# Sparse attention on Trainium2: negated scores, probabilities scaled on GpSimd alone, and one compressed softmax for both token tiles

## The chip, the cores and the metric

The kernel runs on one core of one Trainium2 chip. The metric is the device time of one execution in microseconds (us), the median of several runs. In the profile PE is TensorE (PEld its weight loads), DVE is VectorE, ACT is ScalarE, POOL is GpSimd.

## The reference

The program is three layers over 256 tokens of width 1024: a block of four mixers with an MLP, a retention layer with a gated feed-forward, and a layer of native sparse attention (NSA) with another feed-forward. The change touches only the attention of the NSA layer. With 16 heads in 4 groups, and for each block of 128 queries, it computes:

```
s = einsum(q, kc) + bias                        # 15 compressed keys
p_c = masked_softmax(s, dist_c >= 0);  o_c = einsum(p_c, vc)
s = einsum(q, k_sel) + bias                     # selected blocks
p_s = masked_softmax(s, mask_s);       o_s = einsum(p_s, v_sel)
s = einsum(q, kwin) + bias                      # window
p_w = masked_softmax(s, mask_w);       o_w = einsum(p_w, vwin)
o = gate0 * o_c + gate1 * o_s + gate2 * o_w
```

`masked_softmax` subtracts the row's maximum, takes the exponential and divides by the row's sum (with a floor against rows without any key). At 256 tokens every selected block and the whole window are in reach, so both are plain causal attention with different keys.

## The kernel before, in words

Weights are streamed from HBM as float32 and split into a rounded part (`whi`, L230 on ScalarE) and a remainder (`wlo`, L233 on VectorE), and every projection takes three matmuls (L245 to L247). The function `nsa` first projects keys, values, queries and gates and compresses keys and values; `NSA_ORDER` writes down in which order these pieces and the first score units are issued. Within that, the framework's planner orders the instructions of each engine when the kernel is built, so an engine's order in the trace is not always the order of the source. Each engine then works its own queue in order.

The 16 heads are two pairs of groups (`pair`, 8 heads each: `a` picks the group, `r` one of its four heads). A unit is (pair, token tile `t`, heads `r0` to `r0+nr`, branch `b`: selected or window). There are 12 units, numbered 0 to 11: per pair one of token tile 0 with 4 heads per group and 128 keys, and two of token tile 1 with 2 heads per group and 256 keys, each for both branches. For each unit:

- `u_scores`: TensorE writes the scores into two PSUM banks (L1402, L1403, L1405). VectorE adds the bias table `tz`, writes the sum to SBUF and takes the row maximum in one instruction (L1413, followed by a read of its accumulator), negates the maxima (L1416), ScalarE takes the exponential with the row's sum (L1419), VectorE inverts the sum and multiplies it with the gate (L1421, L1423), and the probabilities are scaled by this row factor (L1425): the half `a = 0` on VectorE, the half `a = 1` on GpSimd.
- `u_weights`: TensorE transposes the probabilities, 4 transposes per half (L1435); ScalarE copies the first half out of PSUM (L1440), VectorE the second (L1438).
- `u_outputs`: TensorE multiplies with the values (L1452); with the window branch it adds the compressed branch from the same bank (L1457), and the result is split into `oT` (L238, L239).

The loop at the end of `nsa` issues in each turn the transposes of unit i, the scores of a later unit, and the outputs of unit i - 1. The compressed softmax (`cmp_softmax`, L1351 to L1377) runs once per pair and token tile: step `S` of the order for pair 0, turn 1 of the loop for pair 1. Its scaling, L1376, is on VectorE. `cmp_weights` (L1379) transposes its result.

After the last unit `project_back` multiplies `oT` with `w_no`.

Of the kernel before, what the change touches and what calls it, by code (L numbers as in the profile page):

```python
# [12 lines left out]
F32 = mybir.dt.float32  # L13
# [3 lines left out]
OP = mybir.AluOpType  # L17
# [6 lines left out]
NEG = -1e30  # L24
# [184 lines left out]
class Kernel:  # L209
# [977 lines left out]
    def nsa(self, inp, xq_pool):  # L1187

        nc, I = self.nc, self.I
        mm = nc.tensor.matmul  # L1190
        rb = self.rb
        with ExitStack() as es:
            cp = self.pool(es, "nc_")
# [3 lines left out]
            tz = cp.tile([128, 16, T], F32, name="tz")  # L1197
# [150 lines left out]
                nc.vector.tensor_scalar(g, g, 1.0, 0.5, op0=OP.add, op1=OP.mult)  # L1348


            def cmp_softmax(pair, t):  # L1351
                nk = 15 if t else 7
                s = cp.tile([128, 8, 32], F32, name=f"sc{pair}{t}")
                nc.gpsimd.memset(s, 0.0)
                sv = s[:, :, 15 - nk:15]

                ps = self.bank()[:, :8 * nk].rearrange("p (r a n) -> p r a n", r=4, a=2)
                for r in range(4):
                    mm(ps[:, r], qT[:, pair * 4 + r, t * 128:(t + 1) * 128], kcz[:, pair, :, 15 - nk:],
                       start=True, stop=True)  # L1360
                for a in range(2):
                    h = pair * 8 + a * 4
                    nc.vector.tensor_tensor(sv[:, a * 4:a * 4 + 4, :], ps[:, :, a, :],
                                            tz[:, h:h + 4, 0:16 * (nk - 1) + 1:16], op=OP.add)
                m = self.st.tile([128, 8], F32, tag="m8", name="m8")
                nc.vector.tensor_reduce(m, sv, AX.X, OP.max)
                nc.vector.tensor_scalar(m, m, -1e25, None, op0=OP.max)
                nc.vector.tensor_tensor(sv, sv, m[:, :, None].to_broadcast([128, 8, nk]), op=OP.subtract)
                nc.scalar.activation(sv, sv, AF.Exp)
                z = self.st.tile([128, 8], F32, tag="z8", name="z8")  # L1370
                nc.vector.tensor_reduce(z, sv, AX.X, OP.add)
                nc.vector.tensor_scalar(z, z, float(np.finfo(np.float32).tiny), None, op0=OP.max)
                rz = self.st.tile([128, 8], F32, tag="rz8", name="rz8")
                nc.vector.reciprocal(rz, z)
                nc.vector.tensor_tensor(rz, rz, gate[:, t, 0, pair * 8:pair * 8 + 8], op=OP.mult)
                nc.vector.tensor_tensor(sv, sv, rz[:, :, None].to_broadcast([128, 8, nk]), op=OP.mult)  # L1376
                return s  # L1377

            def cmp_weights(pair, t, s):  # L1379
                p = self.bank()[:, :256]  # L1380
                for a in range(2):
                    nc.tensor.transpose(p[:, a * 128:(a + 1) * 128],
                                        s[:, a * 4:a * 4 + 4, :].rearrange("p r n -> p (r n)"), self.ident)
# [8 lines left out]
            def u_scores(pair, t, r0, nr, b):  # L1392
                L = 128 * (t + 1)
                ts = slice(t * 128, (t + 1) * 128)
                i = next(nth) % 4
                s = (sp if i < 3 else more[0]).tile([128, 2, nr, L], F32, tag="s", name="s")
                sc = [self.bank().rearrange("p (r k) -> p r k", r=nr) for _ in range(2)]

                for a, i in itertools.product(range(2), range(nr)) if t else [(a, i) for i in range(nr) for a in range(2)]:
                    if t:  # L1400
                        q = qs[a][:, pair, r0 + i]
                        mm(sc[a][:, i, :], q, kh[a][:, b, pair], start=True, stop=False)  # L1402
                        mm(sc[a][:, i, :], q, kl[a][:, b, pair], start=False, stop=True)  # L1403
# [18 lines left out]
                gb = gate[:, t, 1 + b, pair * 8:pair * 8 + 8].rearrange("p (a r) -> p a r", a=2)  # L1422
# [23 lines left out]
            def u_outputs(pair, t, r0, nr, b, pts):  # L1446
# [23 lines left out]
                "S": lambda: sc.update({0: [cmp_softmax(0, t) for t in range(2)]}),  # L1470
# [19 lines left out]
            for i in range(len(units) + 1):  # L1490
                if i < len(units):
                    pts[i] = u_weights(*units[i], ss.pop(i))
                score()
                if i == 0:
                    score()
                if i in (0, 4):
                    for t in range(2):
                        cmp_weights(i // 4, t, sc[i // 4][t])
                if i == 1:
                    sc[1] = [cmp_softmax(1, t) for t in range(2)]  # L1500
                if i:
                    u_outputs(*units[i - 1], pts.pop(i - 1))

# [15 lines left out]
```

## Time and profile before

| | us |
|---|---|
| median of 3 runs | 1227.83 (1225.94 to 1228.5) |
| the profiled execution, its own time | 1227.54 |
| its span in the profile | 1225.8 |
| the attention stage in it | about 940 to 1005.3 |

The granted TensorE clock was full (0.996 in the mean). The span is the time from the first to the last instruction; the stretches below are in us from its start.

### The profile page before, as it was taken

The numbers are of one execution on the slowest core, as the hardware profiler recorded it, in microseconds if no ns is written. First come the engines' busy times: TensorE is split into PE (matmuls) and PEld (weight loads), VectorE is DVE, ScalarE is ACT, GpSimd is POOL, SyncE is SP. The second block draws the span as 40 slices with busy tenths as digits, with TensorE's granted clock in tenths as the row PEclk, the third lists the DMA queues.
The fourth block names the chain that finished last, engine by engine and source line by source line (L and its number), as shares of the span: only waits on it lengthen the run. The fifth ranks groups of instructions, "written<-read, shape, count | busy, mean of one in ns | idle before, by whom it ended". The sixth has DMA issues, their size and how long they took to land.

```text
span 1225.8 us, 20004 instructions
## 1 busy us (share of the span) xinstructions
PE 1202.4 (98%) x7872; PEld 1074.7 (88%) x7872; DVE 775.8 (63%) x1335; ACT 632.2 (52%) x1031; POOL 84.0 (7%) x85
## 2 busy tenths in 40 slices
PE   8999999999999999999999999999999999999997
PEld 6999999997889998899778889999789767899996
DVE  7756866557645557656556655456688977645453
ACT  5544665436544455543545544445577776544441
POOL 1002202100000000012000000000100220000000
PEclk8999999999999999999999999999999999999999
DMA  7554355546455566554446265556654216555560
GB/s 243 188 185 140 104 188 162 167 155 205 163 179 186 184 195 209 190 191 161 161 147 224 98 207 185 187 188 211 200 186 158 71 60 211 177 188 187 182 199 35
DMA packets 60782, 210.22 MB, mean 172 GB/s; under 512 B 7120, under 2 KB 9808, under 8 KB 60560
## 3 DMA queue, kind: packets, MB, share of 16 engines
q1 hardware_dynamic: 60688, 208.95, 52.1%
q8 instruction: 62, 1.02, 0.3%
q14 instruction: 32, 0.26, 0.1%
HBM read 207.84 MB, written 1.08 MB: 170 GB/s over the span
## 4 chain that ended last, share of the span: by engine, by line
PE 85%; DVE 6%; DMA 3%; ACT 3%; issue 1%; POOL 1%; SPq 0%; DVEq 0%; POOLq 0%; ACTq 0%
PE b L245 26%; PE b L246 26%; PE b L247 26%; DVE wlo L233 2%; PE b L408 1%; ACT whi L230 1%; DMA raw<-w_up 1%; PE b L537 1%; DVE s L1413 1%; ACT s L1419 1%; DMA wng<-w_ng 1%; PE b L569 1%; PE b L1081 1%; DMA raw<-w_fi 1%; PE b L588 1%
## 5 line engine op out<-in xcount | busy, mean ns | idle before, releaser
L233 DVE TENSOR_TENSOR wlo<-raw,whi 128x1024 fp32r<-128x1024 f32 (+3 forms) x432 | 473.5, 1108 | 310.4 <-ACT whi L230 307.4
L230 ACT ACTIVATE whi<-raw 128x1024 fp32r<-128x1024 f32 (+1 forms) x384 | 401.3, 1051 | 438.8 <-PE b L246 193.7
L245 PE MATMUL b<-xh,whi 128*128 128x256 f32 x1504 | 428.7, 285 | 0.0
L246 PE MATMUL b<-xl,whi 128*128 128x256 f32 x1504 | 424.6, 282 | 0.0
L247 PE MATMUL b<-xh,wlo 128*128 128x256 f32 x1504 | 424.6, 282 | 0.0
L245 PE MATMUL b<-whi,xh 128*128 128x512 f32 (+1 forms) x752 | 295.8, 395 | 3.0 <-ACT xh L205 2.1
L246 PE MATMUL b<-wlo,xh 128*128 128x512 f32 (+1 forms) x752 | 293.6, 391 | 0.1
L247 PE MATMUL b<-whi,xl 128*128 128x512 f32 (+1 forms) x752 | 291.8, 389 | 0.0
L245 PEld LDWEIGHTS b<-xh,whi 128*128 128x128 f32 x1504 | 287.1, 191 | 3.4 <-issue 2.0
L246 PEld LDWEIGHTS b<-xl,whi 128*128 128x128 f32 x1504 | 287.1, 191 | 1.1
L247 PEld LDWEIGHTS b<-xh,wlo 128*128 128x128 f32 x1504 | 287.1, 191 | 0.0
L245 PEld LDWEIGHTS b<-whi,xh 128*128 128x128 f32 x752 | 141.7, 189 | 36.7 <-ACT xh L205 5.1
L246 PEld LDWEIGHTS b<-wlo,xh 128*128 128x128 f32 x752 | 141.9, 189 | 30.6 <-DVE wlo L233 2.2
L247 PEld LDWEIGHTS b<-whi,xl 128*128 128x128 f32 x752 | 141.7, 188 | 29.5 <-DVE xl L206 0.3
L389 POOL TENSOR_TENSOR rstd<-ms,mhalf 128x1 f32<-128x1 f32 x22 | 14.1, 642 | 692.3 <-DVE ms L387 692.3
L206 DVE SCALAR_TENSOR_TENSOR xl<-b,gc,xh 128x128 fp32r<-128x128 f32 x112 | 36.7, 348 | 19.8 <-ACT xh L205 17.8
L205 ACT ACTIVATE xh<-b,gc 128x128 fp32r<-128x128 f32 x112 | 38.3, 368 | 20.1 <-PE b L408 15.2
L1419 ACT ACTIVATE s<-s,nm 128x128 f32<-128x128 f32 (+1 forms) x64 | 28.2, 442 | 5.8 <-DVE nm L1416 5.7
L582 POOL TENSOR_SCALAR bias<-mk 128x384 f32<-128x384 bf16 x16 | 19.8, 1238 | 119.3 <-DVE m L577 112.2
L239 DVE TENSOR_TENSOR xl<-b,xh 128x256 fp32r<-128x256 f32 (+1 forms) x37 | 17.2, 497 | 7.6 <-ACT xh L238 7.6
L1413 DVE CUSTOM_DVE_ANT_0 s<-b,tz 128x128 f32<-128x128 f32 (+1 forms) x64 | 20.2, 346 | 0.2 <-PE b L1405 0.2
L1047 POOL TENSOR_TENSOR rot<-rot,rotb 128x512 f32<-128x512 f32 x8 | 14.7, 1837 | 76.4 <-DVE rotb L1046 76.4
(264 smaller groups left out, 836.3 us busy)
## 6 DMA issues: line engine op xcount, KB each, us to landing
raw<-w_fi SPq DMA_DIRECT2D x88, 512.0 KB, 3.7
raw<-w_fo SPq DMA_DIRECT2D x44, 512.0 KB, 3.9
raw<-w_gate SPq DMA_DIRECT2D x32, 512.0 KB, 3.9
raw<-w_up SPq DMA_DIRECT2D x32, 512.0 KB, 4.5
raw<-w_down SPq DMA_DIRECT2D x32, 512.0 KB, 4.5
raw<-w_qk SPq DMA_DIRECT2D x24, 512.0 KB, 4.0
raw<-w_rv SPq DMA_DIRECT2D x16, 512.0 KB, 4.9
raw<-w_rqk SPq DMA_DIRECT2D x16, 512.0 KB, 4.6
```

What stands on the lines that cost most here:

```text
L205: k.nc.scalar.activation(hi, ps[:, j, :], AF.Copy, scale=g)
L206: k.nc.vector.scalar_tensor_tensor(lo, ps[:, j, :], g, hi.bitcast(F32), op0=OP.mult, op1=OP.subtract)
L230: nc.scalar.activation(hi[:, :n], r, AF.Copy)
L233: nc.vector.tensor_tensor(lo[:, c], r[:, c], hi[:, c].bitcast(F32), op=OP.subtract)
L239: self.nc.vector.tensor_tensor(lo, src, hi.bitcast(F32), op=OP.subtract)
L245: mm(out, lhs[0], rhs[0], start=start, stop=False)
L246: mm(out, lhs[0], rhs[1], start=False, stop=False)
L247: mm(out, lhs[1], rhs[0], start=False, stop=stop)
L582: nc.gpsimd.tensor_scalar(b, mk[:, kind, :], -slope, None, op0=OP.mult)
L1047: nc.gpsimd.tensor_tensor(a, a, b, op=OP.add)
L1413: nc.vector.tensor_tensor_reduce(s[:, a, i, :], sc[a][:, i, :], tz[:, pair * 8 + a * 4 + r0 + i, :L], 1.0, -3e38, OP.add, OP.max, m[:, a, ...
L1419: nc.scalar.activation(s[:, a, i, :], s[:, a, i, :], AF.Exp, bias=nm[:, a, i:i + 1], accum_out=z[:, a, i:i + 1])
```

## The change

Three edits. The instruction that adds the bias and takes the row maximum now writes the negated sum and takes the row minimum, which is the negated maximum; the exponential then multiplies its input by -1, and the separate negation is gone. Both halves of a unit's probabilities are scaled on GpSimd. The compressed softmax is computed for both token tiles of a pair in one tile of 2 x 8 x 32 columns: the eight keys that token tile 0 lacks are set to -1e30, each step after the bias is issued once over 16 x 15 columns, and its last product is on GpSimd too.

```
-            def cmp_softmax(pair, t):
-                nk = 15 if t else 7
-                s = cp.tile([128, 8, 32], F32, name=f"sc{pair}{t}")
+            def cmp_softmax(pair):
+                s = cp.tile([128, 2, 8, 32], F32, name=f"sc{pair}")
                 nc.gpsimd.memset(s, 0.0)
-                sv = s[:, :, 15 - nk:15]
...
+                nc.gpsimd.memset(s[:, 0, :, :8], NEG)
+                for t in range(2):
+                    nk = 15 if t else 7
...
+                        nc.vector.tensor_tensor(s[:, t, a * 4:a * 4 + 4, 15 - nk:15], ps[:, :, a, :],
+                                                tz[:, h:h + 4, 0:16 * (nk - 1) + 1:16], op=OP.add)
-                m = self.st.tile([128, 8], F32, tag="m8", name="m8")
+                sv = s.rearrange("p t h n -> p (t h) n")[:, :, :15]
+                m = self.st.tile([128, 16], F32, tag="m8", name="m8")
                 nc.vector.tensor_reduce(m, sv, AX.X, OP.max)
                 nc.vector.tensor_scalar(m, m, -1e25, None, op0=OP.max)
-                nc.vector.tensor_tensor(sv, sv, m[:, :, None].to_broadcast([128, 8, nk]), op=OP.subtract)
+                nc.vector.tensor_tensor(sv, sv, m[:, :, None].to_broadcast([128, 16, 15]), op=OP.subtract)
                 nc.scalar.activation(sv, sv, AF.Exp)
...
-                nc.vector.tensor_tensor(rz, rz, gate[:, t, 0, pair * 8:pair * 8 + 8], op=OP.mult)
-                nc.vector.tensor_tensor(sv, sv, rz[:, :, None].to_broadcast([128, 8, nk]), op=OP.mult)
+                rt = rz.rearrange("p (t h) -> p t h", t=2)
+                nc.vector.tensor_tensor(rt, rt, gate[:, :, 0, pair * 8:pair * 8 + 8], op=OP.mult)
+                nc.gpsimd.tensor_tensor(sv, sv, rz[:, :, None].to_broadcast([128, 16, 15]), op=OP.mult)
                 return s
...
-                m = self.st.tile([128, 2, nr], F32, tag="m", name="m")
...
                         nc.vector.tensor_tensor_reduce(s[:, a, i, :], sc[a][:, i, :],
-                                                       tz[:, pair * 8 + a * 4 + r0 + i, :L], 1.0, -3e38,
-                                                       OP.add, OP.max, m[:, a, i:i + 1])
-                nc.vector.tensor_scalar(nm, m, -1.0, None, op0=OP.mult)
+                                                       tz[:, pair * 8 + a * 4 + r0 + i, :L], -1.0, 3e38,
+                                                       OP.add, OP.min, nm[:, a, i:i + 1])
...
                         nc.scalar.activation(s[:, a, i, :], s[:, a, i, :], AF.Exp, bias=nm[:, a, i:i + 1],
-                                             accum_out=z[:, a, i:i + 1])
+                                             scale=-1.0, accum_out=z[:, a, i:i + 1])
...
-                for a, eng in enumerate((nc.vector, nc.gpsimd)):
-                    eng.tensor_tensor(s[:, a], s[:, a], rz[:, a, :, None].to_broadcast([128, nr, L]), op=OP.mult)
+                for a in range(2):
+                    nc.gpsimd.tensor_tensor(s[:, a], s[:, a], rz[:, a, :, None].to_broadcast([128, nr, L]), op=OP.mult)
```

## Rows read from the trace of the kernel before

**Rows 1.** The page, busy time of the engines: busy us (share of the span) x instructions.

```profile
PE 1202.4 (98%) x7872; PEld 1074.7 (88%) x7872; DVE 775.8 (63%) x1335; ACT 632.2 (52%) x1031; POOL 84.0 (7%) x85
```

**Rows 2.** Busy time by stretches: length, busy us (x instructions) per engine, clock, DMA.

```profile
974.90:987.20 12.30, 8.78 (x71) 6.51 (x69) 11.91 (x72) 9.47 (x44) 2.23 (x2) 1.00 0.01 2
...
940.00:1005.30 65.30, 58.73 (x549) 47.61 (x549) 58.52 (x248) 49.37 (x173) 15.52 (x12) 1.00 0.18 58
```

**Rows 3.** TensorE's timeline: start, us, line, out<-in, count [idle before <- releaser].

```profile
950.00 3.15 PE L1335 MATMUL b<-w,hT 128*32 128x64 f32 x64 [1.41 <-DVE hT L1316]
954.46 1.06 PE L1435 MATMUL b<-cm,s 128*128 128x128 f32 x8 [1.31 <-DVE nm L1416]
...
976.46 0.63 PE L1435 MATMUL b<-cm,s 128*128 128x128 f32 x4 [0.90 <-DVE z L1372]
977.62 0.38 PE L1402 MATMUL b<-kh,whi 128*128 128x256 f32 x1 [0.53 <-DVE m L1413]
...
984.30 1.08 PE L1452 MATMUL b<-pt,vn 128*64 128x256 f32 x8 [1.44 <-DVE m L1413]
...
987.18 0.39 PE L1402 MATMUL b<-kh,whi 128*128 128x256 f32 x1 [0.65 <-ACT pct L1385]
```

**Rows 4.** Timeline of VectorE and TensorE, the last two units.

```profile
995.96 0.15 DVE L1423 TENSOR_TENSOR rz<-rz,gate 128x4 f32<-128x4 f32 x1
...
1000.34 0.69 DVE L1425 TENSOR_TENSOR s<-s,rz 128x512 f32<-128x512 f32 x1
...
998.42 1.09 PE L1435 MATMUL b<-cm,s 128*128 128x128 f32 x8
...
1001.99 0.66 PE L1435 MATMUL b<-cm,s 128*128 128x128 f32 x4 [0.18 <-POOL s L1425]
```

**Rows 5.** Timeline of VectorE, instructions with two SBUF operands or few columns.

```profile
952.84 1.47 DVE L1425 TENSOR_TENSOR s<-s,rz 128x512 f32<-128x512 f32 x1
...
958.75 1.57 DVE L233 TENSOR_TENSOR wlo<-raw,whi 128x1024 fp32r<-128x1024 f32 x1
...
968.55 0.69 DVE L1425 TENSOR_TENSOR s<-s,rz 128x512 f32<-128x512 f32 x1
...
971.30 0.72 DVE L1367 TENSOR_SCALAR m<-m 128x8 f32<-128x8 f32 x1
...
973.91 1.01 DVE L1372 TENSOR_SCALAR z<-z 128x8 f32<-128x8 f32 x1
```

**Rows 6.** Timeline of GpSimd.

```profile
952.73 1.04 POOL L1425 TENSOR_TENSOR s<-s,rz 128x512 f32<-128x512 f32 x1 [22.15 <-DVE rz L1423]
...
970.50 1.50 POOL L1425 TENSOR_TENSOR s<-s,rz 128x512 f32<-128x512 f32 x1 [0.36 <-DVE rz L1423]
973.44 1.45 POOL L1425 TENSOR_TENSOR s<-s,rz 128x512 f32<-128x512 f32 x1 [1.45 <-DVE z L1371]
...
1000.48 1.46 POOL L1425 TENSOR_TENSOR s<-s,rz 128x512 f32<-128x512 f32 x1 [2.74 <-DVE rz L1423]
```

**Rows 7.** Timeline of VectorE, short instructions of the first compressed softmax.

```profile
946.99 0.16 DVE L1375 TENSOR_TENSOR rz<-rz,gate 128x8 f32<-128x8 f32 x1
947.07 0.20 DVE L1374 RECIPROCAL rz<-z 128x8 f32<-128x8 f32 x1
947.19 0.22 DVE L1376 TENSOR_TENSOR sc<-sc,rz 128x56 f32<-128x56 f32 x1
```

**Rows 8.** VectorE's groups of instructions: busy us, mean ns | idle before, releaser.

```profile
L233 DVE TENSOR_TENSOR wlo<-raw,whi 128x1024 fp32r<-128x1024 f32 (+3 forms) x432 | 473.5, 1108 | 310.4 <-ACT whi L230 307.4
...
L1413 DVE CUSTOM_DVE_ANT_0 s<-b,tz 128x128 f32<-128x128 f32 (+1 forms) x64 | 20.2, 346 | 0.2 <-PE b L1405 0.2
...
L384 DVE CUSTOM_DVE_ANT_0 junk<-res 128x512 bf16<-128x512 f32 x14 | 9.6, 686 | 2.5 <-DMA res<-x 2.3
```

**Rows 9.** Timeline of ScalarE around the exponentials of unit 6.

```profile
978.34 0.40 ACT L1419 ACTIVATE s<-s,nm 128x128 f32<-128x128 f32 x1 [2.06 <-DVE nm L1416]
...
986.77 0.62 ACT L1385 ACTIVATE pct<-b 128x256 f32<-128x256 f32 x2
```

More of the change, by code (lines that the diff above doesn't have):

```diff
@@ L1348, in gates_back @@
                 nc.vector.tensor_scalar(g, g, 1.0, 0.5, op0=OP.add, op1=OP.mult)
-            def cmp_softmax(pair, t):
-                nk = 15 if t else 7
-                s = cp.tile([128, 8, 32], F32, name=f"sc{pair}{t}")
+            def cmp_softmax(pair):
+                s = cp.tile([128, 2, 8, 32], F32, name=f"sc{pair}")
                 nc.gpsimd.memset(s, 0.0)
-                sv = s[:, :, 15 - nk:15]
[L1357 to L1364, printed above, removed]
-                m = self.st.tile([128, 8], F32, tag="m8", name="m8")
+                nc.gpsimd.memset(s[:, 0, :, :8], NEG)
+                for t in range(2):
+                    nk = 15 if t else 7
+                    ps = self.bank()[:, :8 * nk].rearrange("p (r a n) -> p r a n", r=4, a=2)
+                    for r in range(4):
+                        mm(ps[:, r], qT[:, pair * 4 + r, t * 128:(t + 1) * 128], kcz[:, pair, :, 15 - nk:],
+                           start=True, stop=True)
+                    for a in range(2):
+                        h = pair * 8 + a * 4
+                        nc.vector.tensor_tensor(s[:, t, a * 4:a * 4 + 4, 15 - nk:15], ps[:, :, a, :],
+                                                tz[:, h:h + 4, 0:16 * (nk - 1) + 1:16], op=OP.add)
+                sv = s.rearrange("p t h n -> p (t h) n")[:, :, :15]
+                m = self.st.tile([128, 16], F32, tag="m8", name="m8")
@@ L1366, in cmp_softmax @@
                 nc.vector.tensor_reduce(m, sv, AX.X, OP.max)
                 nc.vector.tensor_scalar(m, m, -1e25, None, op0=OP.max)
-                nc.vector.tensor_tensor(sv, sv, m[:, :, None].to_broadcast([128, 8, nk]), op=OP.subtract)
+                nc.vector.tensor_tensor(sv, sv, m[:, :, None].to_broadcast([128, 16, 15]), op=OP.subtract)
                 nc.scalar.activation(sv, sv, AF.Exp)
-                z = self.st.tile([128, 8], F32, tag="z8", name="z8")
+                z = self.st.tile([128, 16], F32, tag="z8", name="z8")
@@ L1371, in cmp_softmax @@
                 nc.vector.tensor_reduce(z, sv, AX.X, OP.add)
                 nc.vector.tensor_scalar(z, z, float(np.finfo(np.float32).tiny), None, op0=OP.max)
-                rz = self.st.tile([128, 8], F32, tag="rz8", name="rz8")
+                rz = self.st.tile([128, 16], F32, tag="rz8", name="rz8")
                 nc.vector.reciprocal(rz, z)
-                nc.vector.tensor_tensor(rz, rz, gate[:, t, 0, pair * 8:pair * 8 + 8], op=OP.mult)
-                nc.vector.tensor_tensor(sv, sv, rz[:, :, None].to_broadcast([128, 8, nk]), op=OP.mult)
+                rt = rz.rearrange("p (t h) -> p t h", t=2)
@@ L1382, in cmp_weights @@
                     nc.tensor.transpose(p[:, a * 128:(a + 1) * 128],
-                                        s[:, a * 4:a * 4 + 4, :].rearrange("p r n -> p (r n)"), self.ident)
+                                        s[:, t, a * 4:a * 4 + 4, :].rearrange("p r n -> p (r n)"), self.ident)
                 pct[pair, t] = pp.tile([128, 2, 128], F32, name=f"pct{pair}{t}")
@@ L1419, in u_scores @@
                         nc.scalar.activation(s[:, a, i, :], s[:, a, i, :], AF.Exp, bias=nm[:, a, i:i + 1],
-                                             accum_out=z[:, a, i:i + 1])
+                                             scale=-1.0, accum_out=z[:, a, i:i + 1])
+                gb = gate[:, t, 1 + b, pair * 8:pair * 8 + 8].rearrange("p (a r) -> p a r", a=2)
                 nc.vector.reciprocal(rz, z)
-                gb = gate[:, t, 1 + b, pair * 8:pair * 8 + 8].rearrange("p (a r) -> p a r", a=2)
                 nc.vector.tensor_tensor(rz, rz, gb[:, :, r0:r0 + nr], op=OP.mult)
-                for a, eng in enumerate((nc.vector, nc.gpsimd)):
-                    eng.tensor_tensor(s[:, a], s[:, a], rz[:, a, :, None].to_broadcast([128, nr, L]), op=OP.mult)
+                for a in range(2):
+                    nc.gpsimd.tensor_tensor(s[:, a], s[:, a], rz[:, a, :, None].to_broadcast([128, nr, L]), op=OP.mult)
                 return s
@@ L1469, in nsa @@
                 "G": gates, "B": lambda: gates_back(got["G"]),
-                "S": lambda: sc.update({0: [cmp_softmax(0, t) for t in range(2)]}),
+                "S": lambda: sc.update({0: cmp_softmax(0)}),
                 "U0": lambda: ss.update({0: u_scores(*units[0])}), "U1": lambda: ss.update({1: u_scores(*units[1])}),
@@ L1497, in nsa @@
                     for t in range(2):
-                        cmp_weights(i // 4, t, sc[i // 4][t])
+                        cmp_weights(i // 4, t, sc[i // 4])
                 if i == 1:
-                    sc[1] = [cmp_softmax(1, t) for t in range(2)]
+                    sc[1] = cmp_softmax(1)
                 if i:
```

## Prediction

> **What bounds the kernel now.** I read the engine totals first [rows 1]: TensorE shows 98% busy, VectorE 63%, GpSimd 7%. Over the whole span nothing but TensorE could be the limit, and an edit that only relieves VectorE would be worth nothing. So the second view is the table by stretches of the attention stage that the change lies in [rows 2]. Of its 65.3 us VectorE is busy 58.5, and between 974.9 and 987.2 it is busy 11.9 of 12.3 us while TensorE falls to 8.8. There VectorE leads. From 955.3 to 974.9 TensorE has no gap. The third view is TensorE's own order of time [rows 3]: six gaps, 1.41, 1.31, 0.90, 0.53, 1.44 and 0.65 us, together 6.24 of the 6.57 us that it is not busy. That is the ceiling: the matmuls stay what they are, so no relief of another engine can bring more than 6.24 us, 0.5% of the run. What follows the stage starts from its end (the last transposes wait for the last scaled probabilities, [rows 4]), so what is gained at the end of the stage is gained in the run; no DMA is moved.
>
> The fourth view is VectorE beside GpSimd in order of time [rows 5, 6], and it shows what the engine totals hide. GpSimd scales one half in 1.04 us when it is undisturbed. VectorE's own half, 0.69 us when alone (968.55), takes 1.47 at 952.84, and it ends 0.54 us after the GpSimd half that began at 952.73 has ended: it stood still until 953.77. The same holds for small things: the 8-column maximum at 971.30 takes 0.72 us and ends at 972.02, where GpSimd's half (970.50 plus 1.50) ends at 972.00; the one at 973.91 takes 1.01 and ends at 974.92, where GpSimd ends at 974.89. An instruction of that size takes 0.16 otherwise [rows 7]. So these VectorE instructions wait for a GpSimd half to finish, whole, and all that is queued behind them on VectorE waits too. It goes both ways: the half at 970.50 took 1.50.
>
> **The change part by part.** The sum goes against the profiled run, 1227.54 us outside a span of 1225.8; the median of the three runs shown, 1227.83, is 0.29 above it.
>
> *The negated maximum.* L1416 goes, 12 instructions. On so few columns most of the duration is overlapped: L1375, 0.16 us, is followed by the next one 0.08 us after its start [rows 7]. That is 12 x 0.08, about 1 us of VectorE, and one dependent step less ahead of the exponentials. The minimum and the factor -1 replace the maximum and the factor 1 in the same instruction, and the exponential takes its scale as a constant: I count both as 0. The trace has no row of the minimum form. The maximum form costs 20.2 us in 64 instructions [rows 8]; the other end, half its speed, would add 20 us to a VectorE that is full here. A sum of squares under the same name takes 686 ns for 512 columns, the rate of the maxima; so the rate does not hang on which two operations are asked for, and I take 0 and leave that end out of the range.
>
> *One compressed softmax for both token tiles.* Per pair, sixteen VectorE steps after the adds become seven. L1376 goes to GpSimd: 0.14 us for the 56-column form (0.22 less the overlap of 0.08 [rows 7]) and, with about one nanosecond for each further column, 0.20 for the 120-column one. L1375, L1374, L1367 and L1372 are issued once instead of twice: 0.08, 0.12, 0.08, 0.08. The wide steps keep their columns (176 become 240) and are counted as equal. Sum 0.7 us per pair. GpSimd gets 240 columns, estimated as 240/512 of 1.04, 0.5 us, in its queue between two scalings, and one more memset, hidden since GpSimd is idle 93% of the span.
>
> *The first half goes to GpSimd.* VectorE loses 12 times L1425: 0.69 us each when alone, 0.60 after the overlap, more where it was blocked. GpSimd now takes 2 x 1.04 = 2.08 us from the row factor to the second half. The transposes behind it wait for GpSimd alone.
>
> Now where these lie. **(1) The head, 940 to 950.** TensorE waits 1.41 us for the VectorE product of L1316 [rows 3]. Ahead of it the first pair's softmax and one L1416 go: 0.8 us earlier.
>
> **(2) Unit 0, 950 to 955.** Before: GpSimd starts at 952.73, VectorE's blocked half is over at 954.31, eight transposes run from 954.46 to 955.52. After, 0.8 us earlier, GpSimd starts at 951.9 and has its second half at 954.0; its four transposes (half of 1.06) end at about 954.6, 0.9 us earlier. But the next VectorE instruction that blocks is the weight remainder L233, 1.11 us in the mean [rows 8] (a blocked one took the 1.57 of 958.75 [rows 5]): if it gets between the two halves, the second ends 1.1 later, 0.2 us later than before. No row shows who goes first between two GpSimd halves. I take the middle, and (1) and (2) together give -0.3 us.
>
> The Trainium skill, page "SBUF — State Buffer", section "Who interferes with whom", says that the port which VectorE's second SBUF input and GpSimd share is an exclusive lock, and that the order of issue decides who waits. By it a VectorE instruction already waiting goes between the two halves, (1) and (2) would give +0.2 instead of -0.3, and the sum below would be 1226.6. The lock itself is what [rows 5, 6] show; no run here shows the order between two halves.
>
> **(3) The second pair's softmax, 965 to 987.** Its end is set by ScalarE: it starts the exponentials of unit 6 at 978.34, after 2.06 us of waiting for L1416, and works on to the copy of 986.77 [rows 9] for which TensorE waits 0.65 us. So the stretch gains by as much as VectorE is earlier with unit 6's scores. Removed ahead of it: the three L1425 of units 3 to 5 at 0.60, 1.8 us; three L1416, 0.2; the merge, 0.7; the blocking of 971.30 and 973.91, 0.55 + 0.84 = 1.4. Together 4.1. Given back: six short VectorE instructions that block (L1367, L1368, L1372, the gate product of the softmax, and L1423 twice) against a GpSimd that is now busy three pairs and the 240 columns, 6.7 us of 9.4, 0.71 of the time. Each waits between 0 and 1.04 us when it meets one; with half of that, 0.71 x 0.52 x 6 = 2.2 us. Net -1.9. The gaps of 0.90, 0.53 and 1.44 lie inside this stretch and are not counted again.
>
> **(4) 987 to 1000.** TensorE has no gap left here. The tightest unit is the eleventh: its factor is ready at 996.11 and its transposes begin at 998.42 [rows 4], 2.3 us later, so that 2.08 us of scaling lies beside other matmuls; if that cover went, each unit would cost what (5) does.
>
> **(5) The end.** The last unit has nothing behind it to hide in. Before: factor at 1000.3, VectorE's half done at 1001.03, GpSimd's at 1001.94, TensorE waits 0.18 [rows 4]. After: 1000.3 + 2.08 = 1002.4, and the transposes of the second half start about 0.5 later: +0.5.
>
> Sum: -0.3 - 1.9 + 0.5 = -1.7 us, 1225.8 against the profiled run, **1226.1** against the median.
>
> The page "GPSIMD Engine Reference" of the Trainium skill, section "Elementwise — side-by-side cycle accounting", has a two-input product 1.96 times slower on GpSimd than on VectorE. The rows give 1.04 to 0.69, 1.5 times. By the page's ratio a pair would take 2.7 us, (5) would be +1.1 and the sum 1226.7.
>
> **Rivals.** *The relief carries through.* The gaps close because VectorE, relieved of 12 us (12 x 0.69, 12 x 0.16, two merged softmaxes), is no longer late anywhere, and the blocked instructions wait on an engine with slack. For it: VectorE was full, and most of the removed blocking was its own halves. Against it: ScalarE's chain from unit 6 on is 8.7 us long whatever VectorE does. All of 6.24 less 0.5 would give 1222.1; the case spans 1222.1 to 1224.6.
>
> *Nothing comes of it.* Order on the engines is set when the kernel is built, by a planner; it can place other VectorE work where the halves were, and unit 6 starts as before. 1227.0 to 1228.5.
>
> *Slower: VectorE waits behind GpSimd.* The place is (3). If GpSimd keeps the port across its two halves, a blocked instruction waits up to 2.08 us; at 0.71 x 1.04 x 6 = 4.4 the gain of 4.1 is gone, and at most, all 6.7 us of GpSimd's work, (3) costs 2.6. It decides from a mean wait of 0.68 us per blocking instruction on. With 0.3 to 2.6 there, 0.5 at unit 0 and 0.5 at the end: 1229.1 to 1231.4; with a little less of each from 1228.5.
>
> **How the numbers follow.** Chances: my sum, 1224.6 to 1227.0, 0.40; the relief carries through 0.25; nothing 0.17; slower 0.18. This kernel's runs differ by 0.2% between lowest and highest, so less than 0.2% (2.46 us) is no change. Faster than 1225.4 are all of the second case and a third of the first: 0.38. Slower than 1230.3 are about 0.4 of the last: 0.07. Same: 0.55. For the range I leave out the lowest third of the second case (0.08) and the upper two thirds of the last (0.12): 1222.9 to 1229.5.
>
> **What would show it.** Right: VectorE's busy time in the stage falls from 58.5 to about 46; GpSimd scales 24 halves of about 1.04 us; the exponentials of unit 6 start about 2 us earlier than 978.34; the last transposes wait for GpSimd about 0.5 us longer. Wrong: L1423, L1367 or L233 with durations above 1 us in a row (the slower rival), the minimum form slower than the 346 ns of the maximum form, or a stage that is 4 us shorter with no gaps left.

## The result and the profile after

The changed kernel takes **1215.52 us** (median of 4 runs, 1214.44 to 1215.92) against 1227.28 for the kernel before (4 runs, 1225.94 to 1228.5): a ratio of 0.9896, with an interval of 0.9877 to 0.9915, or about -12 us. I had predicted 1226.1, range 1222.9 to 1229.5. The time lies far below the range, and the gain is nearly twice the 6.24 us that the prediction called the most that any relief could bring. The profiled run took 1214.44 us at a span of 1212.6.

The engine totals of the page, after, against [rows 1]:

```profile
PE 1194.9 (99%) x7872; PEld 1071.0 (88%) x7872; DVE 766.5 (63%) x1293; ACT 631.7 (52%) x1029; POOL 96.5 (8%) x99
```

TensorE does the same 7872 matmuls in 7.5 us less busy time (1194.9 instead of 1202.4). That was not in the prediction, which moved only the time between matmuls. The stage by stretches, against the second row of [rows 2], and TensorE's gaps in it, against [rows 3]:

```profile
934.20:993.00 58.80, 56.76 (x548) 47.06 (x548) 48.85 (x206) 48.74 (x170) 27.86 (x26) 1.00 0.20 64
```

```profile
942.97 0.39 PE L247 MATMUL b<-xh,wlo 128*128 128x256 f32 x1 [0.26 <-DVE wlo L233]
...
947.27 3.18 PE L1335 MATMUL b<-w,hT 128*32 128x64 f32 x64 [1.43 <-DVE hT L1316]
...
969.65 0.39 PE L1405 MATMUL b<-kh,whi 128*128 128x256 f32 x1 [0.35 <-ACT pt L1442]
```

The stage lasts 58.8 us instead of 65.3, so 6.5 of the 12 us come from it. The gaps 1.31, 0.90, 0.53, 1.44 and 0.65 are gone; the first, for L1316, is unchanged. VectorE is busy 48.9 us instead of 58.5.

The stage also begins some 5.8 us earlier. I compared the start of each matmul with that of the matmul of the same number before: the lead is 0.15 us at matmul 2000, 1.25 at 2400, 4.25 at 3200 (about 480 us, the end of the first layer's MLP), 5.8 at 6000, just ahead of the stage, 12.4 behind it and 13.2 at the end. Up to the stage TensorE, VectorE and ScalarE have the same instructions in the same order in both traces; of GpSimd's only the clearing of the softmax tiles, at 878 us, differs.

VectorE, GpSimd and ScalarE in the stage, timelines and groups, against [rows 5, 6, 8, 9]. The line numbers have moved: L1416, L1421, L1425, L1427 and L1437 of the changed kernel are L1413, L1419, L1423, L1425 and L1435 of the kernel before.

```profile
950.47 1.22 DVE L233 TENSOR_TENSOR wlo<-raw,whi 128x1024 fp32r<-128x1024 f32 x1
...
952.63 0.97 DVE L1425 TENSOR_TENSOR rz<-rz,gate 128x4 f32<-128x4 f32 x1
```

```profile
950.70 2.89 POOL L1427 TENSOR_TENSOR s<-s,rz 128x512 f32<-128x512 f32 x2 [4.41 <-ACT s L1421]
953.75 3.02 POOL L1427 TENSOR_TENSOR s<-s,rz 128x512 f32<-128x512 f32 x2 [0.16 <-DVE rz L1425]
...
985.54 2.04 POOL L1427 TENSOR_TENSOR s<-s,rz 128x512 f32<-128x512 f32 x2 [1.61 <-DVE rz L1425]
```

```profile
964.44 0.40 ACT L1421 ACTIVATE s<-s,nm 128x128 f32<-128x128 f32 x1 [1.17 <-DVE nm L1416]
```

```profile
L1416 DVE CUSTOM_DVE_ANT_0 s<-b,tz 128x128 f32<-128x128 f32 (+1 forms) x64 | 20.2, 347 | 2.5 <-PE b L1406 2.0 <-PE b L1408 0.4
...
L1427 POOL TENSOR_TENSOR s<-s,rz 128x512 f32<-128x512 f32 x24 | 26.7, 1132 | 15.5 <-ACT s L1421 8.6 <-DVE rz L1425 5.5 <-ACT xh L238 1.2
```

GpSimd's undisturbed pair takes 2.04 us. The one at 950.70 takes 2.89: VectorE's remainder L233 was already running (950.47 to 951.69), and the first half lasts 0.85 us longer. The short gate product L1425 comes up at 952.63, during the second half, and is held for 0.97 until GpSimd ends at 953.59. The minimum form costs what the maximum form did (347 to 346 ns). L1416 now idles for TensorE: VectorE has slack.

The last unit, timeline of VectorE and TensorE, against [rows 4]:

```profile
985.21 0.16 DVE L1425 TENSOR_TENSOR rz<-rz,gate 128x4 f32<-128x4 f32 x1
...
989.49 1.09 PE L1437 MATMUL b<-cm,s 128*128 128x128 f32 x8
```

Its GpSimd pair, the last row of GpSimd above, ends at 987.58; its transposes start 1.9 us later, with no wait listed.

### The profile page after: what moved, and what is told of

The parts are those of the page before. It is cut to its first block, busy times and chain, and to the rows that moved or that the text cites. A ratio compares the mean times of both kernels' runs of the same rounds, so it can differ in the third digit from the quotient of the medians.

```text
span 1212.6 us, 19974 instructions
## 1 busy us (share of the span) xinstructions
PE 1194.9 (99%) x7872; PEld 1071.0 (88%) x7872; DVE 766.5 (63%) x1293; ACT 631.7 (52%) x1029; POOL 96.5 (8%) x99
## 3 DMA queue, kind: packets, MB, share of 16 engines
q8 instruction: 62, 1.02, 0.3%
## 4 chain that ended last, share of the span: by engine, by line
PE 85%; DMA 5%; DVE 4%; ACT 4%; issue 1%; POOL 1%; SPq 0%; DVEq 0%; POOLq 0%; ACTq 0%
PE b L245 25%; PE b L247 25%; PE b L246 25%; DVE wlo L233 2%; ACT whi L230 1%; PE b L408 1%; DMA raw<-w_fi 1%; DMA raw<-w_rv 1%; PE b L537 1%; PE b L1454 1%; PE b L1437 1%; DMA raw<-w_ck 1%; DMA wng<-w_ng 1%; ACT s L1421 1%; PE b L569 1%
## 5 line engine op out<-in xcount | busy, mean ns | idle before, releaser
L233 DVE TENSOR_TENSOR wlo<-raw,whi 128x1024 fp32r<-128x1024 f32 (+3 forms) x432 | 473.3, 1107 | 304.8 <-ACT whi L230 302.2
L245 PE MATMUL b<-xh,whi 128*128 128x256 f32 x1504 | 428.1, 285 | 0.0
L245 PE MATMUL b<-whi,xh 128*128 128x512 f32 (+1 forms) x752 | 294.8, 393 | 3.0 <-ACT xh L205 1.6
L245 PEld LDWEIGHTS b<-xh,whi 128*128 128x128 f32 x1504 | 285.7, 190 | 3.3 <-issue 2.0
L245 PEld LDWEIGHTS b<-whi,xh 128*128 128x128 f32 x752 | 141.5, 188 | 34.7 <-ACT xh L205 4.0
L1421 ACT ACTIVATE s<-s,nm 128x128 f32<-128x128 f32 (+1 forms) x64 | 28.4, 450 | 3.0 <-DVE nm L1416 2.9
L582 POOL TENSOR_SCALAR bias<-mk 128x384 f32<-128x384 bf16 x16 | 19.8, 1238 | 119.3 <-DVE m L577 112.2
L1427 POOL TENSOR_TENSOR s<-s,rz 128x512 f32<-128x512 f32 x24 | 26.7, 1132 | 15.5 <-ACT s L1421 8.6
L1416 DVE CUSTOM_DVE_ANT_0 s<-b,tz 128x128 f32<-128x128 f32 (+1 forms) x64 | 20.2, 347 | 2.5 <-PE b L1406 2.0
```

Of the source, the lines that this page charges most:

```text
L233: nc.vector.tensor_tensor(lo[:, c], r[:, c], hi[:, c].bitcast(F32), op=OP.subtract)
L245: mm(out, lhs[0], rhs[0], start=start, stop=False)
L582: nc.gpsimd.tensor_scalar(b, mk[:, kind, :], -slope, None, op0=OP.mult)
L1427: nc.gpsimd.tensor_tensor(s[:, a], s[:, a], rz[:, a, :, None].to_broadcast([128, nr, L]), op=OP.mult)
```

## The experiments

Two questions: what made unchanged code faster, and how the stage gained 6.5 us where 1.7 were expected. In each table or sentence "before" is the kernel before, timed beside the runs compared with it: 1227.18 us beside the addresses alone, all three edits at the old addresses, the halves alone and the negated minima alone; 1227.01 beside the other rows of the table of edits; 1227.68 beside the three other places; 1227.54 beside the filled head.

### Addresses alone, and the change without them

The change widens the tiles m8, z8 and rz8 of the state pool from 8 to 16 columns: 32 bytes x 3 tiles x 3 buffers = 288 bytes. Every pool opened after it lies 288 bytes higher. By the addresses in the compiled program the MLP's input `xh` moves from byte 132896 to 133184, while the streamed weights stay. The first experiment widens only the tiles of the kernel before; no instruction and no order differs.

```
-                m = self.st.tile([128, 8], F32, tag="m8", name="m8")
+                m = self.st.tile([128, 16], F32, tag="m8", name="m8")[:, :8]
...
-                z = self.st.tile([128, 8], F32, tag="z8", name="z8")
+                z = self.st.tile([128, 16], F32, tag="z8", name="z8")[:, :8]
...
-                rz = self.st.tile([128, 8], F32, tag="rz8", name="rz8")
+                rz = self.st.tile([128, 16], F32, tag="rz8", name="rz8")[:, :8]
```

> The kernel before with nothing changed but the width of three small tiles in the pool st (8 columns allocated as 16), so that each engine has the instructions of before in the order of before, and every tile of a pool opened after st lies 288 bytes higher, where the change puts it. Theory A (the address does part of it: matmuls whose moving tile then lies 64 bytes from a multiple of 128 go from 120 to 114 ns): about 1221.5 us, 5.5 to 6.5 below before, gained between 300 and 480 us and a little in later stages, none of it from the order in the attention stage. Rival B (all of the gain is the attention stage's relief, the earlier difference is one execution's): no change, 1227 us within 0.2%.

Measured: 1221.47 us, ratio 0.9955 (0.9942 to 0.9968), -5.7 us. The second takes the whole change and keeps the pool at its old size: the three tiles share one tag.

```
-                m = self.st.tile([128, 16], F32, tag="m8", name="m8")
+                m = self.st.tile([128, 24], F32, tag="m8", name="m8")[:, :16]
... (z and rz likewise, both with tag="m8")
```

> The whole change, but with the three small tiles of the compressed softmax in one ring of 24 columns, which has the size of the three rings of before, so that every other tile lies where it lay before. Theory A: about 1221 us, 6 to 7 below before, all of it between 940 and 1005, with matmuls of 120 ns between 300 and 480. Rival B: 1215.5 us, as the change.

Measured: 1220.66 us, 0.9943 (0.9931 to 0.9955), -6.5 us. Its lead over before is 0.2 us up to the stage, 6.7 just behind it and 6.95 at the end. So the result has two parts, one of addresses, one of the edits: 5.7 + 6.5 = 12.2 us, measured together 11.8.

### Three other places

If the place counts and not the shift as such, other shifts must give other times. The third widens only m8 (96 bytes), the fourth m8 and z8 (192 bytes), both in the kernel before.

> The kernel before with one of the three state tags (m8) stored 16 columns wide; what is opened behind the state pool lies 96 bytes higher, so that the feed-forward inputs stand on a multiple of 128 bytes, as the streamed weights do. Theory A, phase: the pitch of a matmul follows the place of its two operands modulo 128 bytes. The 768 matmuls of 256 columns keep about 120 ns (119 before; +0.8 us), the 912 of 512 columns go from about 232 to 227 ns (-4.6 us), and 132 others of 512 columns from 233 to 227 (-0.8 us): 1222.6 us, range 1221.5 to 1224. Theory B, any shift helps or wider state tiles do: the whole gain of the run with addresses alone, 1221.5 us, with 256-column matmuls at 114 ns too. Theory C, only the shift of 288 matters: 1227 us.

> The kernel before with two of the three state tags (m8, z8) stored 16 columns wide; what lies behind is 192 bytes higher, at 96 modulo 128, where the few matmuls of the kernel after took 118 to 121 ns at 256 columns. Theory A, phase: 256 columns at 118 to 121 ns and 512 columns at about 232 ns as before: 1227 us, range 1225.5 to 1228.5. Theory B, any shift or wider state tiles: 1221.5 us.

Measured: 1221.98 us, 0.9948 (0.9936 to 0.9959), and 1229.17 us, 1.001 (1.0001 to 1.0019). 96 bytes give as much as 288. 192 bytes cost about 1.5 us: I had expected no change there, and the time lies above my range. The first gains by other matmuls, as theory A says: those of 512 columns, while those of 256 stay at 120 ns. TensorE's timeline in the MLP, matmuls of 512 columns, for before and then for 96 bytes:

```profile
319.48 0.39 PE L245 MATMUL b<-whi,xh 128*128 128x512 f32 x1
...
322.05 0.39 PE L247 MATMUL b<-whi,xl 128*128 128x512 f32 x1
```

```profile
319.63 0.39 PE L245 MATMUL b<-whi,xh 128*128 128x512 f32 x1
...
322.14 0.39 PE L247 MATMUL b<-whi,xl 128*128 128x512 f32 x1
```

Eleven steps take 2.57 us before and 2.51 after the shift: 234 and 228 ns from start to start. The duration shown, 0.39, is the same; only the distance of the starts tells them apart.

The last two move the main layer input alone, the moving operand of 3552 matmuls: padding in front of its pool and behind it, together 256 bytes. One is the changed kernel with 192 bytes in front, one the kernel before with 64. The edit shown is the first one's; the second has 16 columns in front and 48 behind.

```
+            self.pool(es, "pd0", 1).tile([128, 48], F32, name="pd0")
             self.xp = self.pool(es, "xp", 1)
+            self.pool(es, "pd1", 1).tile([128, 16], F32, name="pd1")
             self.st = self.pool(es, "st", 3)
```

> The changed kernel with 192 bytes of padding in front of the pool of the main layer input and 64 behind it, so that only this input changes its place modulo 128 bytes (from 0 to 64); all later tiles keep theirs. It is the moving operand of 3552 matmuls of 256 columns that run at 120 ns. Theory A, phase: they go to 114 ns (-21.3 us), and some 636 matmuls of 512 columns with it as the stationary operand from 227 to about 230 ns (+1.9 us): 1196 us, range 1193 to 1200. Theory D, the 120 ns come from something else in those stages (weight loads, what runs beside): 1215.5 to 1218 us.

> The kernel before with 64 bytes of padding in front of the pool of the main layer input and 192 behind it: only this input changes its place, 64 bytes up. Theory A, with the phase taken modulo 128: 114 ns for its 3552 matmuls of 256 columns, 1227.2 - 21.3 + 1.9 = 1207.8 us, range 1205 to 1212. Theory A2, the phase counts modulo 256 (64 above the weights, as for the 192 matmuls of the kernel before that took 118 ns): 1227.2 - 7.1 + 1.9 = 1222 us. Theory D, the pitch comes from something else in those stages: 1227 to 1230 us.

Measured: **1197.06 us**, 0.9752 (0.974 to 0.9765), which beats both kernels, and 1221.8 us, 0.9954 (0.9942 to 0.9967). Theory A is met by the first, theory A2 (modulo 256) by the second. TensorE's timeline at 100 us in before, with 192 bytes (changed kernel), and with 64:

```profile
99.72 0.28 PE L245 MATMUL b<-xh,whi 128*128 128x256 f32 x1
...
100.80 0.28 PE L245 MATMUL b<-xh,whi 128*128 128x256 f32 x1
```

```profile
99.83 0.28 PE L247 MATMUL b<-xh,wlo 128*128 128x256 f32 x1
...
100.85 0.28 PE L247 MATMUL b<-xh,wlo 128*128 128x256 f32 x1
```

```profile
99.82 0.28 PE L246 MATMUL b<-xl,whi 128*128 128x256 f32 x1
...
100.88 0.28 PE L246 MATMUL b<-xl,whi 128*128 128x256 f32 x1
```

Nine steps each: 120, 113 and 118 ns. The next table goes by the distance of the moving from the stationary operand's address modulo 256 bytes. Each entry is one large group of matmuls (636 to 4320) in one of the kernels before and after and the last four: start to start in ns, median (mean, with longer waits cut at 400 ns), all at a mean granted clock of 0.996 or more:

| distance | 256 columns, layer input moving | 512 columns, weights moving |
|---|---|---|
| 0 | 120 (120.9) | 227 (230.4) |
| 64 | 118 (118.9) | 229 (230.8) |
| 96 | 119 (120.6) | 232 (234.3) |
| 160 | 119 (119.3) | 234 (235.4) |
| 192 | 113 (115.4) | 233 (235.5) |

For 512 columns the rows speak for the distance and not for the place of one operand: in before, by the same addresses, inputs that lie at 32 modulo 256 give 227 ns with weights at 32 too (287 matmuls) and 232 with weights at 128 (912). For 256 columns the weights lie at 128 in every run, so that the distance and the input's own place cannot be told apart.

With these means the sums come out to within 0.4 to 2 us. Addresses alone: 768 matmuls from 160 to 192 (119.3 to 115.5 in that kernel) give -2.9 us, 912 from 96 to 64 (234.3 to 230.6) give -3.4, together -6.3, measured -5.7. The 192 bytes in front of the main input: 3552 x -5.5 ns = -19.5 and 636 x +0.9 = +0.6; measured -18.5 against the changed kernel, which was timed separately. For the 64 bytes: -7.1 and +3.2 = -3.9, measured -5.9. For the state pool's 96 bytes: 768 matmuls from 160 to 0 (+1.2), 912 from 96 to 0 (-3.6) and 132 from 160 to 0 (-1.4, from 241.0 ns there) give -3.8, measured -5.7; for its 192 bytes +1.0 and +1.0 = +2.0, measured +1.5. The two sums for 64 and 96 bytes leave 2 us that the table does not explain.

The Trainium skill, page "SBUF — State Buffer", section "Who interferes with whom", gives TensorE two read ports, one for the moving operand and one for the weight load, independent of each other. These runs agree with that only in part: at 512 columns the pitch goes with how the two operands lie to each other (227 to 234 ns), and the measurement decides. Why it is so no view shows.

### The three edits, singly and in pairs

All at the old addresses. The edits are those of the diff ahead of the prediction, singly or with one left out.

> Of the change only the scaling of both halves on GpSimd, at the old addresses. Theory A1 (this part is the stage's gain, because VectorE's halves stood still behind GpSimd's): 4 to 5 us below before, TensorE's gaps of 1.44 and 0.90 us gone. Rival A2 (the parts are worth something only together, since the second pair's softmax still waits behind GpSimd): within 2 us of before. Rival A3 (blocked short VectorE instructions take the gain): slower than before.

> Of the change only the negated sum with the row minimum, at the old addresses. Theory A1: 0.5 to 1.5 us below before (12 short instructions on VectorE less), the minimum form at the 346 ns of the maximum form. Rival A4 (one step less ahead of the exponentials starts ScalarE earlier in every unit and is the larger part): 3 us or more below before.

> Of the change only the merged compressed softmax with its product on GpSimd, at the old addresses; negation and VectorE's halves as before. Theory C1 (the parts add up, and the other two alone were worth nothing): about 6.5 us below before. Theory C2 (the merged softmax lets the planner put 24 instead of 2 of the last query projection's matmuls ahead of the compressed values, which fills TensorE's wait, and the GpSimd halves take the later gaps): 2 to 3.5 below, the gap of 1.31 gone, the gaps of 0.90, 0.53, 1.44 and 0.65 mostly still there. Rival C3 (the merge is worth something only with GpSimd's halves): within 1 us of before.

> Negation and both halves on GpSimd, two softmaxes per pair as before, at the old addresses. C1: within 1 us of before. C2: within 2 us of before, since the order of the projection's matmuls stays that of before (2 ahead of the compressed values). C3: within 1.5 us of before.

> Merged softmax and both halves on GpSimd, the maximum negated by an instruction of its own as before, at the old addresses. C1, C2 and C3: 5.5 to 6.5 us below before, the negation being worth less than 1 us. If the negation is what starts ScalarE early enough: only 3 to 4 below.

> Merged softmax and negation, VectorE scaling its half as before, at the old addresses. C1: 6 to 7 us below before. C2: 2.5 to 4 below, VectorE's halves blocked behind GpSimd's as before (1.2 to 1.5 us each) and TensorE's gaps in the second pair still there. C3: within 1.5 us of before.

| edits in | us | ratio to before | interval |
|---|---|---|---|
| both halves on GpSimd | 1226.69 | 0.9993 | 0.9984 to 1.0002 |
| negated minima | 1227.74 | 1.0008 | 0.9996 to 1.002 |
| merged softmax | 1225.59 | 0.9987 | 0.9978 to 0.9996 |
| GpSimd and negated | 1226.67 | 0.9995 | 0.9986 to 1.0004 |
| GpSimd and merged | 1224.16 | 0.998 | 0.9971 to 0.9989 |
| negated and merged | 1223.39 | 0.9971 | 0.9959 to 0.9982 |
| all three | 1220.66 | 0.9943 | 0.9931 to 0.9955 |

The single gains sum to 1.3 us, all together bring 6.5. That the parts add up is refuted (theory C1), and so is A1: the halves alone gain 0.5 and the negation nothing, as A2 had it for the halves. The merge alone gains 1.4, between C3 and C2; GpSimd and merged 2.9, far from the 5.5 to 6.5 expected and just short of the 3 to 4 named for a negation that counts; negated and merged 3.6, as C2 had it. TensorE's timeline shows where the gain of the pairs goes, first its gaps with GpSimd and negated, without the merge:

```profile
953.29 5.78 PE L1335 MATMUL b<-w,hT 128*32 128x64 f32 x64 [4.65 <-DVE hT L1316]
981.82 0.38 PE L1402 MATMUL b<-kh,wlo 128*128 128x256 f32 x1 [0.36 <-ACT pt L1438]
```

With GpSimd and merged, without the negated minima (the last two of six gaps):

```profile
983.29 0.63 PE L1439 MATMUL b<-cm,s 128*128 128x128 f32 x4 [0.59 <-DVE rz L1427]
984.90 0.39 PE L1405 MATMUL b<-kh,whi 128*128 128x256 f32 x1 [0.98 <-ACT pct L1388]
```

With all three, all gaps:

```profile
952.68 3.18 PE L1335 MATMUL b<-w,hT 128*32 128x64 f32 x64 [1.44 <-DVE hT L1316]
975.05 0.38 PE L1405 MATMUL b<-kh,whi 128*128 128x256 f32 x1 [0.26 <-ACT pt L1442]
```

Without the merge the later gaps of [rows 3] are gone too, so the relief works. But the wait at the head has grown from 1.41 to 4.65 us. Both orders come from the planner. With the negated minima VectorE's timeline has 30 and 32 rows of score minima, accumulator reads among them, ahead of `hT` in the two kernels without the merge, where the kernel before has 18; so `hT` comes 3.4 us later. And without the merge 2 of the last query projection's 48 matmuls stand ahead of L1335 on TensorE, with it 24 (26 in one kernel). With all three `hT` is as late (952.35 to 952.97), but TensorE has those 22 matmuls to do meanwhile.

The longer wait costs more than itself: the 64 matmuls behind it take 5.78 us, not 3.18. The same kernel by stretches of 2 us:

```profile
950.00:952.00 2.00, 0.00 (x0) 0.00 (x0) 1.94 (x6) 1.95 (x9) 1.91 (x2) 1.00 0.02 4
952.00:954.00 2.00, 0.71 (x7) 0.71 (x8) 1.97 (x10) 2.00 (x12) 0.31 (x1) 0.61 0.00 0
954.00:956.00 2.00, 2.00 (x28) 2.00 (x28) 2.00 (x7) 2.00 (x10) 0.00 (x0) 0.50 0.03 8
...
958.00:960.00 2.00, 2.00 (x20) 1.83 (x17) 1.15 (x2) 0.87 (x3) 2.00 (x2) 0.69 0.85 285
```

TensorE stood idle for 4.65 us, and from the end of that idle time the granted clock shows the lower of its two levels, 0.50, until about 959. In the kernel before it waited 1.41 us there and the clock stayed at 1.00.

### The idle time at the head filled

Whether the low clock costs the run anything was tested by filling the idle time with 24 transposes of the identity that do no work of the reference: in the kernel without the merge, in that with the negated minima alone, and in the kernel before.

```
-                p = self.bank()[:, :T].rearrange("p (g d) -> p g d", g=4)
+                b = self.bank()
+                for i in range(24):
+                    nc.tensor.transpose(b[:, :128], self.ident, self.ident)
+                p = b[:, :T].rearrange("p (g d) -> p g d", g=4)
```

> The kernel with both halves on GpSimd and negated minima, without the merge, at the old addresses (1226.67 us), with 24 transposes of the identity put into the idle time of TensorE ahead of the compressed values; they write a bank that is overwritten and do no work of the reference. In the kernel without them TensorE is idle for 4.65 us there, its granted clock then stands at 0.50 for some 5.5 us, and the 64 small matmuls behind take 5.78 us, not 3.15. Theory E, the clock: with 2.6 of the 4.65 us filled the clock stays at full, the 64 matmuls take 3.2 us, and the run gains 2.6 us: 1224.1, range 1223.3 to 1225. Theory F, the low clock costs nothing because VectorE sets the time behind it: 1226.7, range 1226 to 1227.5.

> The kernel with the negated minima alone (1227.74 us) with the same 24 transposes. Its idle time there is 4.72 us, the 64 matmuls behind take 4.76 us at a granted clock of 0.50 and then full. Theory E: they take 3.2, and the run gains 1.6 us: 1226.1, range 1225.3 to 1227. Theory F: 1227.7, range 1227 to 1228.5.

> Control: the kernel before with the same 24 transposes. Its idle time there is 1.41 us at full clock, so that they only delay the 64 matmuls by 1.2 us, which lies in the 1.31 us that the next transposes wait for VectorE: 1227.7, range 1226.7 to 1229 by both theories. If it is faster by 1 us or more, the transposes help in another way than theory E says.

Measured, against 1227.54 us: 1224.37 us, 0.9976 (0.9966 to 0.9985); 1227.98 us, 0.9998 (0.9989 to 1.0007); 1226.42 us, 0.9993 (0.9984 to 1.0002). TensorE in the first:

```profile
946.65 2.78 PE L1333 MATMUL b<-cm 128*128 128x128 f32 x24
951.27 3.18 PE L1338 MATMUL b<-w,hT 128*32 128x64 f32 x64 [1.84 <-DVE hT L1316]
```

The clock stays at 1.00 and the run gains 2.3 us (2.6 expected). Its stage, from the first L1359 to the first L245 behind, is shorter by as much in the profiled executions, 65.0 and 62.8 us. Theory E's forecast is met here.

The second run misses theory E's range: the 64 matmuls take 3.18 us there too, but 1227.98 us is no gain on 1227.74. The trace says something else. First and last row of the stage, negated minima alone, then filled (L1362 is L1359 there):

```profile
939.74 1.87 PE L1359 MATMUL b<-kcz,qT 128*128 128x14 f32 x16
...
1006.48 0.51 PE L245 MATMUL b<-whi,xh 128*128 128x512 f32 x1
```

```profile
940.73 1.87 PE L1362 MATMUL b<-kcz,qT 128*128 128x14 f32 x16
...
1005.82 0.50 PE L245 MATMUL b<-whi,xh 128*128 128x512 f32 x1
```

The stage takes 66.7 and 65.1 us, the 1.6 less that theory E forecast; the filled execution lost 1.0 us ahead of the stage and 1.2 behind it, where nothing had been changed. The two ratios to before, 1.0008 (0.9996 to 1.002) and 0.9998, leave room for both theories. TensorE's waits for VectorE behind stay (0.46 and 0.82 before and after the filling), but they do not take the gain back. In the stage theory E's figure is met here too; in the time of the run it is not shown.

The control lies 1.1 us below before, under its range, which I had named as a sign that the transposes help in another way too. Its interval includes no change, and its profiled stage is only 0.16 us shorter (65.14 to 64.98). So the 2.3 us are the clock's by the stage's rows, with up to 1.1 us in doubt by the times.

So the three belong together in this way. Without GpSimd's second half the other two bring 3.6 of the 6.5 us, and TensorE has six listed waits, 2.8 us together, in the place of the 1.7. The negated minima take a step out of VectorE's chain (without them TensorE has six listed waits, 3.2 us together, three of them for VectorE's maxima and one for its row factor) but come with an order that puts `hT` later. The merge comes with an order that gives TensorE 22 matmuls to do until then, and with it the wait and the clock stay as before (1.44 us, 1.00). Of the 6.0 us that are missing without the merge the filling brought back 2.3; the other 3.7 stand beside a wait that is 3.2 longer. A run with the planner's order held fixed while the merge is taken out was not tried, so that the order's share is argued, not shown.

### Who goes first between two halves

The run with only the halves moved answers what the prediction had left open. Its GpSimd and VectorE, then TensorE:

```profile
953.61 3.02 POOL L1425 TENSOR_TENSOR s<-s,rz 128x512 f32<-128x512 f32 x2 [22.22 <-DVE rz L1423]
953.72 2.01 DVE L233 TENSOR_TENSOR wlo<-raw,whi 128x1024 fp32r<-128x1024 f32 x1
```

```profile
954.70 0.65 PE L1435 MATMUL b<-cm,s 128*128 128x128 f32 x4 [0.67 <-POOL s L1425]
956.68 0.66 PE L1435 MATMUL b<-cm,s 128*128 128x128 f32 x4 [1.32 <-POOL s L1425]
```

L233 comes up at 953.72, while the first half runs, and has the port between the two: it ends at 955.73 and the pair takes 3.02 us instead of 2.04. TensorE waits 1.32 us for the second half. That the one issued first goes first is what the Trainium skill states (page "SBUF — State Buffer", section "Who interferes with whom"), and the trace agrees: 2.01 us for L233 and 3.02 for the pair. In the changed kernel the same happens to the pair at 953.75 (3.02 us, above), and no wait of TensorE is listed for it. VectorE's row beside it:

```profile
954.47 1.40 DVE L233 TENSOR_TENSOR wlo<-raw,whi 128x1024 fp32r<-128x1024 f32 x1
```

## Why the prediction was wrong, point by point

- **The ceiling of 6.24 us** is the step that failed, in two ways. "The matmuls stay what they are" took equal instructions for equal time. The widened tiles moved the operands of some 2000 matmuls against each other: 5.7 us, shown by the run with addresses alone. And the sum of the listed gaps was no limit for the stage either. At the old addresses TensorE's idle time there fell by 4.9 us (6.57 of 65.3 to 1.71 of 58.8) and its busy time by 1.6 (58.73 to 57.09):

```profile
939.70:998.50 58.80, 57.09 (x550) 47.40 (x549) 48.89 (x206) 48.74 (x170) 27.83 (x26) 1.00 0.19 65
```

Matmuls that start 0.12 us apart are shown 0.28 long, so a wait of up to 0.16 us between two counts as busy; that the 1.6 us are such waits is my reading. The stage gained 6.5, hardly more than 6.24 (the run's interval is 5.5 to 8.5).

- **The sum of the stage, -1.7,** was mis-sized in every term. At the old addresses TensorE's lead over before grows from 0.2 to 1.2 us by unit 1's transposes (-1.0 where (1) and (2) had -0.3), to 5.3 at the L1402 of 987.18 (-4.1 where (3) had -1.9), to 6.1 at 999.58 (-0.9 where (4) had 0) and to 6.7 behind the stage (-0.5 where (5) had +0.5). Unit 1's transposes before, then those and the L1402 at the old addresses (L1405 there):

```profile
963.15 1.04 PE L1435 MATMUL b<-cm,s 128*128 128x128 f32 x8
```

```profile
961.95 1.04 PE L1437 MATMUL b<-cm,s 128*128 128x128 f32 x8
...
981.92 0.36 PE L1405 MATMUL b<-kh,whi 128*128 128x256 f32 x1
```

- **(1) and (2), the head.** VectorE's earlier product was expected; the wait for it stayed (1.41 to 1.43). What went with the gain was the planner's new order on TensorE, which I had seen as a rival, and only as a loss. VectorE's remainder did go between two halves, and cost no listed wait.
- **(3).** Its sign and engine were right: in the run at the old addresses unit 6's exponentials start at 969.84 instead of 978.34 [rows 9], 8.5 us earlier where I had 2. VectorE's busy time fell to 48.9 (predicted about 46). The 2.2 us given back to the port were not seen: gate products are held for up to 0.98 us, but VectorE has slack now (it waits 2.5 us for TensorE at L1416).
- **(4), 0:** no gap is left there, as expected, and yet 0.9 us of lead are gained, without a listed wait to show where.
- **(5), +0.5,** did not come. I let the last unit's transposes wait for GpSimd, as before [rows 4]. But then TensorE is the late one: it gets to them 1.9 us after GpSimd is done.
- **The negated minimum at no extra cost** was right: 347 ns to 346. **GpSimd's 24 halves** took 1132 ns in the mean, 1.02 undisturbed (2.04 a pair).
- **The Trainium skill's ratio of 1.96** (page "GPSIMD Engine Reference", section "Elementwise — side-by-side cycle accounting"), which that page gives for an addition over 2048 columns, did not show for this product over 512: 1.02 to VectorE's 0.69 us [rows 5] is 1.5. By it the sum was 1226.7, further off than my own.
- **The rivals.** "The relief carries through" was the right one for the stage: behind the head no listed wait of TensorE is for VectorE. At the old addresses it gives 1220.66 instead of its 1222.1 to 1224.6, because it was bounded by the same ceiling. No rival spoke of addresses.

## What to carry to other kernels

Before you take the code ahead of a change for unchanged, compare tile addresses as well as instructions: widening a small tile in a pool that is opened early moves everything opened behind it, and a run with the addresses alone separates that from the edit at the cost of three changed lines. When TensorE is the bound, look at the distance of the starts of its matmuls, not at their durations, and try shifts of the operands: padding in front of one pool brought 18.5 us, more than the whole change. And test edits to one engine's chain together too: a relief that comes with a longer wait of TensorE can be lost twice, where the clock falls with the wait.

## What the runs showed of the hardware that I had not expected

The pitch of equal matmuls at full clock goes with where the moving and the stationary operand lie: 113 to 120 ns for 256 columns and 227 to 234 ns for 512, by the table above, with the best distance for the one (192 bytes) among the worst for the other. Idle times of 4.65 and 4.72 us on TensorE went with some 6.8 and 3.4 us at the granted clock of 0.50, the lower of its two levels (worked out from the mean clocks of 2 us slices), idle times of 1.41 and 1.84 us in the same place with none. The length of the idle time alone does not decide: in the run with only the halves moved, 50 us ahead of the stage, one of 1.76 us was followed by some 3.4 us at 0.50. TensorE's row behind it and two slices:

```profile
889.12 0.51 PE L245 MATMUL b<-whi,xh 128*128 128x512 f32 x1 [1.76 <-ACT xh L205]
```

```profile
890.00:892.00 2.00, 2.00 (x7) 1.61 (x6) 1.81 (x4) 0.53 (x3) 0.00 (x0) 0.59 0.00 0
892.00:894.00 2.00, 2.00 (x6) 1.53 (x6) 0.57 (x1) 1.57 (x4) 0.00 (x0) 0.56 0.65 217
```
